# Reciprocal square roots of eighteen norms: Newton steps on VectorE or one power on GpSimd

## The chip, the cores and the metric

The kernel runs on one core of a Trainium2 chip, in one launch. The metric is the device time of a run in microseconds (us). Where several runs were made, the median stands beside the lowest and the highest.

## The reference, cut to what matters

Two streams of tokens, 512 latent and 256 context, 1024 channels each, pass through two layers. A layer norms the stream, projects it into four groups of columns, runs a mixer on each group (SSD, Hyena, retention, S5), projects the four outputs back, and ends with a gated feed-forward stage that is normed too. What the change touches is the factor of each norm:

```python
def rms_norm(x, g):
    xf = x.astype(jnp.float32)
    y = xf * lax.rsqrt(jnp.mean(xf * xf, axis=-1, keepdims=True) + EPS)
    return (y * g.astype(jnp.float32)).astype(x.dtype)

def retention_out(y, g):
    ...
    yn = ((yf - mu) * lax.rsqrt(var + EPS)).astype(g.dtype)
    return (jax.nn.silu(g) * yn).reshape(g.shape[0], g.shape[1], W_GRP)
```

`rms_norm` stands at the two norms of a layer, at the output of the SSD mixer and at the end of the program. The second layer needs no context output, so a few of its context norms are left out.

## The kernel before, in words

Activations lie with channels on the 128 partitions and tokens along the free axis, eight tiles of 128 channels for a stream. Every product of float32 operands is made of three passes of TensorE on rounded high and low parts: ScalarE rounds a tile to its high part (`act`, line 155), VectorE or GpSimd subtracts to get the low part (`sub` over `tt`, line 134). Weights come by SyncE's DMA queue into a staging ring `wst` (line 207) and are split in the same way into `whi` and `wlo`. All matmuls have line 126 and accumulate in PSUM banks of four rings (`ps_mm`, `ps_xa`, `ps_xb`, `ps_md`).

A norm has these steps. The squares of the eight tiles are added into `acc`. TensorE sums `acc` over the partitions with one matmul per 128 tokens against a column of ones (`ps_xa<-const,acc`; in the SSD mixer `sz` stands for `acc`, in the retention `rq`). VectorE scales the sums and adds epsilon, which gives the small tile `rv` (in the retention `rrv`): 128 tokens on the partitions by 2 or 4 groups of tokens, 8 or 16 columns in the retention. `rsq` (line 188) replaces that tile by its reciprocal square root. TensorE then spreads it over all partitions with matmuls against the identity (`ps_xa<-const,rv`), and VectorE multiplies the tiles by the spread row (`nt` in the two norms of a layer, `sin` in the SSD mixer, `ry` in the retention, `xl` in the final norm of `finish`). ScalarE and the low-part subtractions make the operands `ahl`, `alol` (latent) and `ahc`, `aloc` (context) of the next products.

`rsq` takes an integer estimate and three Newton steps, twelve VectorE instructions on the small tile, each of which needs the one before or one of the two before:

```python
self.ts(i, v.bitcast(I32), 1, op0=ALU.logical_shift_right)
self.ts(i, i, -1.0, float(0x5F3759DF), ALU.mult, ALU.add)
self.ts(h, v, -0.5)
y = i.bitcast(F32)
for _ in range(3):
    self.mul(t, y, y)
    self.mul(t, t, h)
    self.stt(v, t, 1.5, y, ALU.add, ALU.mult)
    y = v
```

It is called eighteen times: twice in `start` (context, then latent input), eight times from `norm_seg` (three after the first output projection, three at the entry of the second layer, two after the second output projection; a call takes 256 tokens), three times each in `ssd` and `ret`, and twice in `finish`.

`start` (from line 427) also makes the modulation: weights `wst<-in_wm_dram` go straight to TensorE as `ps_md<-wst,csil`, ScalarE copies the row (`mrow`), TensorE turns it into a column, VectorE adds the bias (`modv`), and only then are two channel tiles of each stream normed. The ring `ps_md` has one bank. Beside that, VectorE makes the tables of the S5 mixer's rotations (`rot`, `rotT`, `rotw`, `s5z`, `early`), which are read later.

The order of the instructions on each engine is not the order of the code. A scheduler places them by the priorities given in the code and by its own estimates of when operands are ready, so another instruction at one place can shift its neighbours on every engine. Each engine then runs its row in order and waits at a row whose operands are missing. Buffers of a ring and PSUM banks add waits of the same kind.

Of the kernel before, what the change touches and what calls it, by code (L numbers as in the profile page):

```python
# [33 lines left out]
def halves(a):  # L34
    """A table as two float32 parts that float32r carries exactly."""
    def keep12(x):
        u = np.ascontiguousarray(x, np.float32).view(np.uint32).astype(np.uint64)
        return ((u + 2047 + ((u >> 12) & 1)) >> 12 << 12).astype(np.uint32).view(np.float32)
    hi = keep12(a)
    return np.ascontiguousarray(np.stack([hi, keep12(a - hi)], 1))  # L40
# [66 lines left out]
class Kern:  # L107
# [7 lines left out]
    def at(self, p):  # L115
        """Instructions in this block get priorities from p on."""
# [44 lines left out]
    def pst(self):  # L161
        """A PSUM bank from the ring of the current flow of work."""
# [5 lines left out]
    def pst2(self, fl="mm+xb"):  # L168
        """As pst, from two rings in turn where no mixer runs."""
# [6 lines left out]
    def flow(self, fl, p=None):  # L176
        """Work that takes its banks and small tiles from rings of its own; p: its priority."""
# [10 lines left out]
    def rsq(self, v, n):  # L188
        """v: (128, n) tile, replaced by 1/sqrt(v)."""
        i = self.sm.tile([128, 24], I32, tag="rq_i" + self.fl[:2], name="rq_i", bufs=2)[:, :n]  # L190
        h = self.sm.tile([128, 24], F32, tag="rq_h" + self.fl[:2], name="rq_h", bufs=2)[:, :n]
        t = self.sm.tile([128, 24], F32, tag="rq_t" + self.fl[:2], name="rq_t", bufs=2)[:, :n]
        self.ts(i, v.bitcast(I32), 1, op0=ALU.logical_shift_right)
        self.ts(i, i, -1.0, float(0x5F3759DF), ALU.mult, ALU.add)
        self.ts(h, v, -0.5)
        y = i.bitcast(F32)
        for _ in range(3):
            self.mul(t, y, y)
            self.mul(t, t, h)
            self.stt(v, t, 1.5, y, ALU.add, ALU.mult)  # L200
            y = v

    def piece(self, src, nk, ncol):
        """src: (128, nk * ncol) of a weight laid out by pieces."""
# [5 lines left out]
    def weights(self, srcs, nk=8):  # L210
        """Pieces of 128 columns as high and low parts."""
# [7 lines left out]
    def held(self, src):  # L219
        """Four tiles of rows of a weight with all its columns, src: (8, 128, 512)."""  # L220
# [20 lines left out]
    def bulk(self):  # L241
        """Products that fill the tensor engine come after the mixers' own."""
# [34 lines left out]
    def put_y(self, s, k, t, c0=0):  # L277
        """Keep tile k of the mixers' output: as operands of the output projection where these have room already."""
# [12 lines left out]
    def ytiles(self, s, p):  # L291
        """Tiles that are not written in the order of their making: each has its own place."""
# [3 lines left out]
    def prep(self):  # L296
# [5 lines left out]
        nc.scalar.dma_start(k, A["c_const"])  # L302
        self.ident = k[:, 0:128]
# [30 lines left out]
    def mod(self, i, c0, c1):  # L334
        """Columns 256*c0 .. 256*c1 of the modulation of layer i."""
# [15 lines left out]
    def mod_vec(self, i, cols, both, p):  # L351
        """As mod for tiles of columns, with a column of the weights a row: products and sums on VectorE.
        The context stream has the tiles in both only."""
# [16 lines left out]
    def gains(self, i, part, s, gat):  # L370
        """(1 + scale) * g for a stream; part is 1 or 4."""
# [4 lines left out]
    def sq_acc(self, s, x, acc, first):  # L376
        """acc += x*x"""
# [7 lines left out]
    def rinv_rows(self, s, accs, scale, c0=0, c1=None):  # L385
        """Per-token 1/sqrt(scale * sum over channels + eps), broadcast to all partitions in PSUM."""
# [14 lines left out]
    def segs(self, s):  # L401
        """Ranges of tokens that are normed one after the other, so that products of one hide the norm of the next."""
# [23 lines left out]
    def start(self):  # L426
        """Norm of the inputs and the first two blocks of columns of the first layer's input projection,
        by pairs of channel tiles as their modulation arrives."""
# [1474 lines left out]
```

## Time and profile before

| what | value |
|---|---|
| median of 3 runs | 1917.07 us |
| lowest and highest run | 1908.82 and 1919.6 us |
| profiled execution: span from its first to its last instruction | 1919.5 us |
| profiled execution: time of its own, apart from the span | none is listed |
| TensorE matmuls busy | 1790.1 us (93%) |
| VectorE busy | 1257.5 us (66%), 2941 instructions |
| ScalarE busy | 713.5 us (37%) |
| GpSimd busy | 207.3 us (11%), 273 instructions |
| mean granted TensorE clock | 0.960 of full speed |

An engine's busy time is a sum over stages that have different limits. What an edit in one stage is worth is read where an engine waits: the timeline prints, behind an instruction, how long its engine sat idle before it and what ended that. PE is TensorE, PEld its weight loads, DVE VectorE, ACT ScalarE, POOL GpSimd, SP SyncE.

### The profile page before, as it was taken

Reading aid. Unit: us, or ns where it says so; the run is one execution under the profiler, and the core shown is the slowest. Engines: PE = TensorE matmul, PEld = TensorE weight load, DVE = VectorE, ACT = ScalarE, POOL = GpSimd, SP = SyncE. Lnnn points to the kernel's source line nnn. Section 1 sums busy time; section 2 is a strip of 40 time slices with the busy share of each in tenths; the row PEclk is TensorE's granted clock in tenths of the full one; section 3 lists DMA queues with packets and bytes.
Section 4 is the critical chain, followed back from the end, with each engine's and each line's share of the span. In section 5 each row is a group of like instructions: output and inputs, shape, how many; then the busy total and the mean of one; then the engine's idle time right before and its main releaser. Section 6 shows DMA issues by size and latency. Waiting matters only on the chain.

```text
span 1919.5 us, 28992 instructions
## 1 busy us (share of the span) xinstructions
PE 1790.1 (93%) x10792; PEld 1526.3 (80%) x10792; DVE 1257.5 (66%) x2941; ACT 713.5 (37%) x1390; POOL 207.3 (11%) x273
## 2 busy tenths in 40 slices
PE   3789878898999999999999999989999999999997
PEld 2678767686789888888888989878866888888886
DVE  8788764778858899777665427678576843233336
ACT  4354234555227223212132115514673542222222
POOL 0201121123002000011223000121110000000000
PEclk9899979998899999999999999999997999999998
DMA  6656588765612335656635513565563322222331
GB/s 231 178 138 186 149 180 229 243 192 160 203 56 89 121 123 164 219 190 230 210 113 131 155 44 123 158 207 159 153 201 96 126 73 94 89 96 88 97 101 56
DMA packets 193089, 280.87 MB, mean 146 GB/s; under 512 B 51745, under 2 KB 127837, under 8 KB 192436
## 3 DMA queue, kind: packets, MB, share of 16 engines
q1 hardware_dynamic: 107188, 166.20, 28.5%
q10 hardware_dynamic: 55920, 64.72, 10.9%
q0 software_dynamic: 29840, 48.09, 8.9%
q8 instruction: 85, 1.39, 0.3%
q14 instruction: 56, 0.46, 0.1%
HBM read 235.00 MB, written 43.96 MB: 145 GB/s over the span
## 4 chain that ended last, share of the span: by engine, by line
PE 58%; DVE 11%; issue 8%; DMA 8%; ACT 3%; POOL 1%; ACTq 0%; SPq 0%; DVEq 0%; POOLq 0%
PE ps_mm L126 31%; PE ps_xb L126 20%; PE ps_xa L126 4%; DMA mvw<-in_wmt_dram 4%; PE ps_md L126 2%; DMA wst<-in_wi_dram 1%; ACT L155 1%; DVE mvo L364 1%; DVE wlo L134 1%; DVE gt L134 1%; DVE t L134 1%; DVE g L1499 1%; DVE cst L134 1%; DVE s5tmp L134 1%; ACT whi L155 1%
## 5 line engine op out<-in xcount | busy, mean ns | idle before, releaser
L155 ACT ACTIVATE whi<-wst 128x1024 fp32r<-128x1024 f32 (+3 forms) x226 | 198.9, 917 | 361.5 <-PE ps_mm L126 169.4
L134 DVE TENSOR_TENSOR wlo<-wst,whi 128x1024 fp32r<-128x1024 f32 (+3 forms) x226 | 233.9, 1058 | 83.5 <-ACT whi L155 81.2
L126 PE MATMUL ps_mm<-alol,whi 128*128 128x512 f32 (+1 forms) x688 | 262.7, 383 | 0.4 <-POOL alol L134 0.4
L126 PE MATMUL ps_mm<-ahl,wlo 128*128 128x512 f32 (+1 forms) x688 | 262.3, 382 | 0.0
L126 PE MATMUL ps_mm<-ahl,whi 128*128 128x512 f32 (+1 forms) x688 | 260.9, 383 | 0.3 <-ACT ahl L155 0.2
L126 PE MATMUL ps_mm<-h,whi 128*128 128x512 f32 (+1 forms) x592 | 168.8, 365 | 0.9 <-DVE h L134 0.7
L126 PE MATMUL ps_xb<-ahl,whi 128*128 128x512 f32 (+1 forms) x416 | 154.2, 373 | 3.8 <-ACT ahl L155 3.8
L126 PE MATMUL ps_xb<-ahl,wlo 128*128 128x512 f32 (+1 forms) x416 | 153.8, 370 | 0.0
L126 PE MATMUL ps_xb<-alol,whi 128*128 128x512 f32 (+1 forms) x416 | 153.5, 371 | 0.1
L134 DVE TENSOR_TENSOR sg<-sg,ps_mm 128x512 f32<-128x512 f32 (+1 forms) x70 | 39.9, 570 | 172.9 <-PE ps_mm L126 172.7
L126 PEld LDWEIGHTS ps_mm<-alol,whi 128*128 128x128 f32 x688 | 130.7, 190 | 26.4 <-issue 2.7
L126 PEld LDWEIGHTS ps_mm<-ahl,wlo 128*128 128x128 f32 x688 | 130.7, 190 | 24.5 <-issue 1.1
L126 PEld LDWEIGHTS ps_mm<-ahl,whi 128*128 128x128 f32 x688 | 130.2, 191 | 25.0 <-issue 1.6
L126 PE MATMUL ps_xb<-h,whi 128*128 128x256 f32 (+1 forms) x592 | 129.2, 310 | 0.1
L364 DVE SCALAR_TENSOR_TENSOR mvo<-mvw,crow 128x1024 f32<-128x1024 f32 x80 | 97.8, 1222 | 39.6 <-DMA mvw<-in_wmt_dram 38.7
L126 PE MATMUL ps_mm<-ahc,whi 128*128 128x256 f32 x368 | 107.4, 296 | 13.0 <-ACT whi L155 8.6
L126 PEld LDWEIGHTS ps_mm<-h,whi 128*128 128x128 f32 x592 | 103.7, 188 | 17.5 <-DVE h L134 1.2
L126 PE MATMUL ps_mm<-aloc,whi 128*128 128x256 f32 x368 | 108.2, 295 | 1.0 <-DVE aloc L134 1.0
L126 PE MATMUL ps_mm<-ahc,wlo 128*128 128x256 f32 x368 | 107.1, 293 | 2.0 <-DVE wlo L134 2.0
L126 PEld LDWEIGHTS ps_xb<-h,whi 128*128 128x128 f32 x592 | 98.9, 188 | 11.6 <-issue 1.1
L126 PE MATMUL ps_mm<-h,wlo 128*128 128x512 f32 (+1 forms) x296 | 107.9, 365 | 0.0
L155 ACT ACTIVATE h<-sg 128x512 fp32r<-128x512 f32 (+1 forms) x70 | 37.4, 534 | 161.7 <-DVE sg L134 161.6
(576 smaller groups left out, 4137.3 us busy)
## 6 DMA issues: line engine op xcount, KB each, us to landing
wst<-in_wu_dram SPq DMA_DIRECT2D x88, 512.0 KB
mvw<-in_wmt_dram POOLq DMA_DIRECT2D x56, 512.0 KB, 3.7
wst<-in_wi_dram SPq DMA_DIRECT2D x42, 512.0 KB
wst<-in_wm_dram SPq DMA_DIRECT2D x40, 512.0 KB
wst<-in_wd_dram SPq DMA_DIRECT2D x24, 384.0 KB
ftab<-in_c_ftL_dram POOLq DMA_DIRECT2D x32, 256.0 KB, 5.0
wst<-in_wd_dram SPq DMA_DIRECT2D x32, 256.0 KB
s5rot<-s5r SPq DMA_DIRECT2D x32, 192.0 KB
```

The source lines that it names most:

```text
L126: return self.nc.tensor.matmul(out, lhsT, rhs, start=start, stop=stop)
L134: return (eng or self.nc.vector).tensor_tensor(out, a, b, op=op)
L155: return self.nc.scalar.activation(out, in_, func, bias=bias, scale=scale)
L364: self.nc.vector.scalar_tensor_tensor(o, st, 1.0, crow[:, q], op0=ALU.mult, op1=ALU.mult, accum_out=mv[:, c, q:q + 1])
L1499: nc.vector.tensor_tensor_scan(o, dcy, x, 0.0, ALU.mult, ALU.add)
```

## The change

`rsq` becomes a single GpSimd instruction that raises the small tile to the power of a constant tile, and that constant tile of minus one half is made once at the start. Twelve VectorE instructions at each of eighteen places go, one GpSimd instruction comes.

```diff
     def rsq(self, v, n):
-        i = self.sm.tile([128, 24], I32, tag="rq_i" + self.fl[:2], name="rq_i", bufs=2)[:, :n]
-        h = self.sm.tile([128, 24], F32, tag="rq_h" + self.fl[:2], name="rq_h", bufs=2)[:, :n]
-        t = self.sm.tile([128, 24], F32, tag="rq_t" + self.fl[:2], name="rq_t", bufs=2)[:, :n]
-        self.ts(i, v.bitcast(I32), 1, op0=ALU.logical_shift_right)
-        self.ts(i, i, -1.0, float(0x5F3759DF), ALU.mult, ALU.add)
-        self.ts(h, v, -0.5)
-        y = i.bitcast(F32)
-        for _ in range(3):
-            self.mul(t, y, y)
-            self.mul(t, t, h)
-            self.stt(v, t, 1.5, y, ALU.add, ALU.mult)
-            y = v
+        self.tt(v, v, self.mhalf[:, :n], ALU.pow, self.nc.gpsimd)
...
         nc.scalar.dma_start(k, A["c_const"])
+        self.mhalf = cp.tile([128, 24], F32, name="mhalf")
+        nc.gpsimd.memset(self.mhalf, -0.5)
```

The scheduler gives the rest of the program a new order. Of 9,733 matmul instructions that both programs have, 1,261 stand elsewhere relative to the others, by at most 104 places. On GpSimd the old rows keep their order but for five. Three places show what moved.

The first is VectorE in `start`, at the first norm's way to its first use. Before, the last of the rows between the second Newton step's end and the first `nt` product (`rot` and `rotT` are rotation tables, `wlo` low parts of weights, `early` S5 powers) read:

```order
L152 SCALAR_TENSOR_TENSOR rv<-rq_t,rv 128x2
L134 TENSOR_TENSOR rotT<-rot,rotw 128x128
L134 TENSOR_TENSOR rot<-rot,rotw 128x128
L134 TENSOR_TENSOR rotw<-rotw 128x16
L134 TENSOR_TENSOR rot<-rot,rotT 128x128
```

In the changed order the rows that end with the first two `nt` products are:

```order
L152 SCALAR_TENSOR_TENSOR rotw<-rotw 128x16
L134 TENSOR_TENSOR wlo<-wst,whi 128x8x128
L149 TENSOR_SCALAR rv<-ps_xa 128x4
L134 TENSOR_TENSOR early<-early,s5T 128x256
L134 TENSOR_TENSOR rotT<-rot,rotw 128x32
L134 TENSOR_TENSOR rot<-rot,rotw 128x64
L134 TENSOR_TENSOR nt<-xc,pb 128x256 x2
```

From the row that makes the context's `rv` to the first `nt` product 77 rows lie between before and 24 now; the rotation rows that stood in front now stand behind.

The second is TensorE at the end of the second layer's mixers, where the retention's factors are spread (`ps_md<-const,rrv`) and the SSD mixer's sums and factors follow (`CE` are decays of the entering states, `yhl` and `yol` the operands of the output projection). Before:

```order
L126 MATMUL ps_xa<-CE,Hn 64x128 x8
L126 MATMUL ps_xb<-const,rq 128x2 x2
L126 MATMUL ps_xa<-CE,Hn 64x128 x8
L126 MATMUL ps_md<-const,rrv 64x128 x8
L126 MATMUL ps_xb<-const,rrv 64x128 x8
L126 MATMUL ps_xa<-const,sz 128x1 x8
L126 MATMUL ps_md<-yhl_13753,whi 128x512
```

Now, first the retention's rows and then, some eighty rows on, the SSD mixer's:

```order
L126 MATMUL ps_xa<-sin 128x128
L126 MATMUL ps_md<-const,rrv 64x128 x8
L126 MATMUL ps_xb<-const,rrv 64x128 x8
L126 MATMUL ps_xa<-vd,Bt 64x256
L126 MATMUL ps_xa<-E,xt 64x128 x4
L126 MATMUL ps_md<-yhl_13587,whi 128x512
```

```order
L126 MATMUL ps_mm<-yhl_13590,wlo 128x256
L126 MATMUL ps_xa<-const,sz 128x1 x8
L126 MATMUL ps_xa<-const,rv 128x128 x4
L126 MATMUL ps_xb<-yhl_13585,whi 128x256
```

The retention's factors are spread before the SSD mixer's last products with `CE`, and products of the output projection fill the rows in between; the SSD mixer's own factor now stands directly behind its sums, with the products that read its tiles (`yhl_13585`) directly behind that.

The third is VectorE at the end of the program, where the second half's last products are added (`xl<-ps_mm,modv`), its squares summed (`acc`), and the first half is multiplied by its factor (`xl<-xl,vec,ps_xa`). Before:

```order
L152 SCALAR_TENSOR_TENSOR xl<-ps_mm,modv_87,xl 128x256
L152 SCALAR_TENSOR_TENSOR xl<-xl,vec,ps_xa 128x256 x8
L134 TENSOR_TENSOR acc<-acc,sq 128x256
L149 TENSOR_SCALAR rv<-ps_xa 128x2
```

Now:

```order
L152 SCALAR_TENSOR_TENSOR xl<-xl,vec,ps_xa 128x256 x4
L152 SCALAR_TENSOR_TENSOR xl<-ps_mm,modv_89,xl 128x256
L152 SCALAR_TENSOR_TENSOR xl<-xl,vec,ps_xa 128x256 x4
L152 SCALAR_TENSOR_TENSOR xl<-ps_xb,modv_89,xl 128x256
L134 TENSOR_TENSOR acc<-acc,sq 128x256
L152 SCALAR_TENSOR_TENSOR xl<-ps_mm,modv_89,xl 128x256
L134 TENSOR_TENSOR acc<-acc,sq 128x256 x2
L149 TENSOR_SCALAR rv<-ps_xa 128x2
```

The eight products of the first half's final norm stood behind the last row that reads TensorE; now they stand three such rows earlier.

## Rows read from the trace of the kernel before

**Rows 1.** The page: its span and the line of busy times.
```profile
span 1919.5 us, 28992 instructions
PE 1790.1 (93%) x10792; PEld 1526.3 (80%) x10792; DVE 1257.5 (66%) x2941; ACT 713.5 (37%) x1390; POOL 207.3 (11%) x273
```

**Rows 2.** Busy time by stretch; columns: stretch, length, engines, clock, DMA share, GB/s.
```profile
0.00:50.00 50.00, 18.72 (x108) 11.63 (x109) 42.45 (x252) 22.89 (x50) 1.49 (x7) 1.00 0.65 235
600.00:700.00 100.00, 100.00 (x661) 91.89 (x661) 86.19 (x298) 36.27 (x80) 9.44 (x14) 1.00 0.29 93
1550.00:1900.00 350.00, 350.00 (x1607) 286.62 (x1606) 129.04 (x166) 91.84 (x124) 0.00 (x0) 1.00 0.28 89
```

**Rows 3.** One tile's instructions, rq_t: count, shortest/median/longest ns, first and last start.
```profile
L134 DVE TENSOR_TENSOR rq_t<-rq_t,rq_h x54: 146/161/665, 33.8 to 1911.4; 128x2 f32<-128x2 f32 x36, 128x4 f32<-128x4 f32 x9, 128x16 f32<-128x16 f32 x6, 128x8 f32<-128x8 f32 x3
```

**Rows 4.** Timeline, first norm: start, duration, instruction, idle before it and releaser.
```profile
30.94 0.15 DVE L149 TENSOR_SCALAR rv<-ps_xa 128x2 f32<-128x2 f32 x1
...
35.11 1.21 DVE L134 TENSOR_TENSOR wlo<-wst,whi 128x1024 fp32r<-128x1024 f32 x1
...
39.35 0.80 PE L126 MATMUL ps_xa<-const,rv 128*128 128x128 f32 x2 [9.13 <-DVE rv L152]
...
42.78 0.42 DVE L134 TENSOR_TENSOR nt<-xc,pb 128x256 f32<-128x256 f32 x1
...
44.75 0.65 PE L126 MATMUL ps_md<-wst,csil 128*32 128x256 f32 x4 [0.71 <-DVE modv L134]
```

**Rows 5.** The same stretch: busy times of four microseconds, and SP's next weight loads.
```profile
36.00:40.00 4.00, 0.65 (x3) 0.65 (x4) 4.00 (x28) 0.00 (x0) 0.00 (x0) 1.00 0.00 0
...
45.89 1.49 SPq L207 DMA_DIRECT2D wst<-in_wm_dram  x2
```

**Rows 6.** Timeline, TensorE at the retention's factors of context, layer 1.
```profile
496.31 1.98 PE L126 MATMUL ps_mm<-const,rrv 128*64 128x128 f32 x16 [3.23 <-DVE rrv L152]
```

**Rows 7.** Timeline, TensorE at the end of the second layer's mixers.
```profile
1482.08 1.12 PE L126 MATMUL ps_xa<-CE,Hn 128*64 128x128 f32 x8 [4.45 <-DVE rrv L152]
```

**Rows 8.** Timeline before the second layer's feed-forward stage, and a stretch as in Rows 2.
```profile
1518.02 0.16 DVE L149 TENSOR_SCALAR rv<-ps_xa 128x2 f32<-128x2 f32 x1 [0.18 <-PE ps_xa L126]
...
1526.34 0.68 PE L126 MATMUL ps_xa<-const,rv 128*128 128x128 f32 x4 [1.07 <-DVE rv L152]
1529.66 0.58 PE L126 MATMUL ps_xb<-ahl,whi 128*128 128x256 f32 x1 [2.64 <-ACT ahl L155]
...
1528.00:1532.00 4.00, 2.28 (x9) 1.99 (x10) 4.00 (x8) 3.46 (x8) 1.92 (x2) 0.52 0.58 170
```

**Rows 9.** Timeline, the end of the program.
```profile
1904.11 0.61 PE L126 MATMUL ps_xa<-const,rv 128*128 128x128 f32 x4
1908.46 0.98 PE L126 MATMUL ps_xa<-const,acc 128*128 128x1 f32 x4 [3.74 <-DVE acc L134]
1911.95 1.20 PE L126 MATMUL ps_xa<-const,rv 128*128 128x128 f32 x4 [2.51 <-DVE rv L152]
...
1904.76 3.22 DVE L152 SCALAR_TENSOR_TENSOR xl<-xl,vec,ps_xa 128x256 f32<-128x256 f32 x8
```

**Rows 10.** Groups by shape: count, busy us, mean ns, idle before and releaser.
```profile
L134 POOL TENSOR_TENSOR alol<-nt,ahl 128x256 fp32r<-128x256 f32 x24 | 19.0, 790 | 123.6 <-ACT ahl L155 123.6
L1885 POOL MEMSET const-float32-0.0<- 128x1 f32 x1 | 0.1, 99 | 0.3 <-issue 0.3
...
L134 DVE TENSOR_TENSOR alol<-nt,ahl 128x256 fp32r<-128x256 f32 x24 | 12.4, 518 | 4.8 <-ACT ahl L155 4.6
```

**Rows 11.** Timeline: a hand-off from VectorE to GpSimd, and GpSimd's first arithmetic.
```profile
357.24 0.68 DVE L134 TENSOR_TENSOR t<-vp,Ft 128x512 f32<-128x512 f32 x1
...
358.07 1.06 POOL L134 TENSOR_TENSOR t<-t,t 128x256 f32<-128x256 f32 x1 [0.77 <-DVE t L134]
...
44.91 0.73 POOL L134 TENSOR_TENSOR aloc<-nt,ahc 128x256 fp32r<-128x256 f32 x1 [43.55 <-ACT ahc L155]
```

**Rows 12.** The chain that ended last, in order of time: start, us, what.
```profile
1901.43 1.43 PE ps_xb L126 x12
```

## The prediction

> **What bounds the kernel now.** I read the page's busy times first, then busy time by stretch, then the timeline around each of the eighteen norms. TensorE is busy for 1790.1 of 1919.5 us [rows 1], so all that an edit elsewhere can give back is some 130 us of TensorE's idle time, plus matmuls that ran at a lower clock behind such idle time. Two of the long stretches show TensorE busy without a gap (100.00 of 100.00 us from 600, 350.00 of 350.00 us from 1550) [rows 2]; a norm that falls there costs nothing now, however long its chain. The first 50 us are another matter: TensorE 18.72 us busy, VectorE 42.45 [rows 2]. So the question is at which of the eighteen places TensorE stands still because of the Newton steps.
>
> It does at six. In `start` the context's sums are turned into `rv` at 30.94, and TensorE spreads it at 39.35 after 9.13 us of idleness that VectorE's `rv` ended [rows 4]. A lone chain of twelve takes about 2.1 us; here its rows were queued among rotation tables and low parts. TensorE's next instructions are behind it, the modulation among them, which runs at 44.75 [rows 4], so no weight buffer comes free: the DMA share of 36 to 40 us is 0.00 and the next weight loads are issued at 45.89 [rows 5]. The retention of the context stream holds TensorE for 3.23 us [rows 6], the end of the second layer's mixers for 4.45 us [rows 7], the norm ahead of the last feed-forward stage for 1.07 and then 2.64 us [rows 8], and the end of the program for 3.74 and 2.51 us [rows 9].
>
> **The change, part by part.** *Removed:* 12 x 18 = 216 VectorE instructions of about 0.161 us [rows 3], some 35 us of VectorE's 1257.5. Where TensorE has no gaps this is worth nothing, since VectorE has room there (86.19 of 100, 129.04 of 350) [rows 2]. I count it at nothing except where VectorE is the engine that is late.
>
> *Added:* eighteen powers and one fill of a small tile. No row shows a power on GpSimd. From below it costs the 0.10 us of the smallest fill; from above, twelve steps at the 0.79 us of a subtraction of 128x256 would be 9.5 us [rows 10]. I take 0.8 us: a subtraction over 256 columns fits into 0.79 us, and a power has 2 to 16 columns and perhaps a dozen or two elementary steps for each, so the same number of steps. The new path is then: VectorE's `rv` 0.16, hand-off to GpSimd 0.15 (357.24 + 0.68 to 358.07 [rows 11]), the power 0.8, hand-off to TensorE about 0.15, in all 1.3 us against 2.5 for a lone chain [rows 9].
>
> GpSimd works at 790 ns where VectorE takes 518 for the same shape [rows 10]. The Trainium skill's page "GPSIMD Engine Reference", section "Engine selection", says to keep elementwise arithmetic on VectorE, because GpSimd takes about twice as long for operations with two inputs. The trace agrees in direction, with a ratio of 1.5. By that rule alone the change loses at every place; by the rows one instruction stands against twelve, so the ratio would have to exceed about twelve.
>
> *GpSimd's queue:* each power stands where its operand is due. At the entry of the feed-forward stages it stands behind four low parts of the segment before, which end ahead of the old time of spreading, so I count that wait at nothing; the cover is the product work in TensorE's queue. Its DMA issues (the modulation weights of the second layer) move behind the context's power by less than the old order made them wait.
>
> *Covered places:* in the changed order eleven norms have 20 to 37 matmuls between sums and spreading, mostly 28. At 1.43 us for 12 [rows 12] 28 last 3.3 us, above the path of 1.3. They cost and give nothing.
>
> *The first norm.* `rv` ready at 30.94 + 1.3 is spread at about 32.2 instead of 39.35. Next VectorE is late: 24 rows lie before the first `nt` now. The second `wlo` starts at 35.11 before [rows 4]; less six Newton rows spaced 0.08 us and plus four short rows behind it, `nt` starts at about 36.4, not 42.78. The modulation, and with it the loads of 45.89 [rows 5], come about 6.5 us earlier. But the rotation rows that stood in front follow behind, and VectorE is busy throughout (4.00 of 4.00 [rows 5]). If it stays the bound, only the 24 Newton rows of both norms are won, 24 x 0.075 = 1.8 us; if its later gaps take in the tables, 6.7 us. Taken: 4.5.
>
> *The retention of the context:* 2.5 us becomes 1.3; 1.2 won (0 to 1.5).
>
> *The end of the second layer's mixers.* The 4.45 us [rows 7] go, since the retention's spreading no longer follows the products with `CE`. What is late next is the SSD mixer: its factor is spread right behind its sums and its tiles are read right behind that, so 1.3 us of path, about 0.7 for the product and 0.6 for the rounding lie open. Won: 4.45 - 2.6, less 0.4 for the spreading itself, 1.5 (-1 to 4.5).
>
> *The norm before the last feed-forward stage.* Twelve rows among sums and `wlo` took from 1518.02 to 1526.34 [rows 8]. With a path of 1.3 us and 28 matmuls as cover, the operands are ready when TensorE arrives, and 1.07 + 2.64 us go; behind that gap the granted clock was 0.52 [rows 8], which lost another 1 to 3 us. Taken: 4 (1 to 7).
>
> *The end.* Before, TensorE ends its products at 1904.1, the eight products of the first half take 3.22 us on VectorE and the last sum waits for them; TensorE idles 3.74 us [rows 9]. Now these products start once 28 matmuls have passed, with some 3.1 us of matmuls left; about 5.4 us of VectorE rows then end 2.3 us behind TensorE instead of 4.2, less 0.2 for the spreading moved: 1.7 won. The lone chain gives 2.5 - 1.3 = 1.2. Together 2.9 (0 to 5.5).
>
> **The sum.** 4.5 + 1.2 + 1.5 + 4 + 2.9 = 14.1 us, with ends of about 3 and 25. Against the profiled execution: 1919.5 - 14.1 = 1905.4. The median of the runs lies 2.4 us below its span, so for a median I forecast **1903 us**. About 0.5% (9.6 us) is what a measurement of this kernel can tell from no change.
>
> **The rivals.**
>
> *The power is long (slower).* GpSimd would have to take more than about 2.8 us, so that 2.8 + 0.5 us of hand-offs outlast the 3.3 us of the 28 matmuls. From there each of the eleven covered places holds TensorE for the excess, and four open ones for what passes 2 us. At 4.5 us that is 11 x 1.7 + 4 x 2.5 = 29 us less some 4 still won at the first norm: 25 slower, about 1942; at the upper end of 9.5 us about 2020. For it: nothing in the trace prices the operation. Against it: the sizes are 2 to 16 columns, and 0.79 us buys 256 subtractions.
>
> *VectorE or the loads are the bound anyway.* The stalls go, but the next wait takes their place: 1.8 at the first norm, 1.2, 0, 1 and 2.9 at the others, 6.9 in all, about 1910. For it: VectorE without a gap in `start` [rows 5], and `wlo` rows in the queue before the feed-forward stage. The new order elsewhere can add or take a few us with either sign.
>
> *The first power is slow to begin.* If code for it had to be loaded when first called, the first norm would be spread about when it is now, and 4.5 us less are won: about 1907.5. Against it: GpSimd's first arithmetic instruction took 0.73 us, like later ones [rows 11]. The Trainium skill's page "GPSIMD Engine Reference", section "Instruction dispatch", puts such a load at roughly 6 us for the first call of a freshly loaded routine. By that figure the sum would be the same 1907.5 or so; the trace shows no such delay for a subtraction.
>
> That the change does not do what it says is out: its VectorE order has no Newton rows left, and its GpSimd order has eighteen powers.
>
> **How the numbers follow.** My forecast has 0.54 (own range 1894 to 1912), the bound elsewhere 0.24 (1905 to 1922), the slow first call 0.06, the long power 0.16 (1922 to 2020). The range is 1894 to 1922: it leaves out the long power and the far end of the largest gains, 2 in 10. Faster by over 0.5% (below 1907.5): four fifths of the forecast, half of the slow first call, a little of the second rival, 0.50. Slower by over 0.5% (above 1926.7): nearly all of the long power, 0.16. The rest, 0.34, lies between.
>
> **What would show it.** In the profile of the changed kernel a power group on GpSimd of 18 instructions should have a mean near 0.8 us; above 2.8 the first rival holds. The wait of TensorE at the first spreading should fall from 9.13 to about 2 us and the third pair of weight loads should be issued near 39 instead of 45.89. TensorE's gap ahead of the last feed-forward stage should be under 1 us with the clock at 1.00 there. VectorE's busy time should fall by about 35 us, and TensorE's stretches without gaps should stay so. I am wrong if TensorE waits for GpSimd at the covered places, or if the first modulation comes early and the first products of the feed-forward stage or of the second block of columns do not.

## The result, and the profile after

| | before | changed |
|---|---|---|
| median of 9 runs | 1917.07 us | 1926.58 us |
| lowest and highest | 1908.82 and 1919.84 us | 1920.95 and 1936.18 us |
| span of the profiled execution | 1919.5 us | 1926.7 us |

The ratio is 1.0052, with a 95% interval of 1.0035 to 1.007: half a per cent slower, 4.6 us beyond the upper end of the range.

The page of the changed kernel, against [rows 1]:

```profile
span 1926.7 us, 28815 instructions
PE 1790.1 (93%) x10792; PEld 1523.7 (79%) x10792; DVE 1228.1 (64%) x2725; ACT 711.5 (37%) x1390; POOL 235.4 (12%) x292
```

TensorE is busy for the same 1790.1 us as before. All of the 7.2 us by which the spans differ is TensorE's idle time, although VectorE lost 29.4 us of work. The powers, in GpSimd's groups by shape (count, busy us, mean ns, idle before and releaser):

```profile
L134 POOL TENSOR_TENSOR rv<-rv,mhalf 128x2 f32<-128x2 f32 x12 | 9.6, 799 | 479.7 <-DVE rv L149 448.9 <-DVE s5z L134 30.8
L134 POOL TENSOR_TENSOR rrv<-rrv,mhalf 128x16 f32<-128x16 f32 x2 | 5.8, 2914 | 72.8 <-DVE rrv L148 72.8
L134 POOL TENSOR_TENSOR rv<-rv,mhalf 128x4 f32<-128x4 f32 x3 | 3.2, 1072 | 55.5 <-DVE rv L149 55.5
L134 POOL TENSOR_TENSOR rrv<-rrv,mhalf 128x8 f32<-128x8 f32 x1 | 1.6, 1637 | 8.3 <-DVE rrv L148 8.3
```

The guess of 0.8 us holds for two columns and not beyond: each further column adds about 0.15 us ((2.914 - 0.799) / 14).

**Where the time goes.** To see at which place the executions part, I lined them up by the work that TensorE had done: every matmul counted at the shortest spacing that its form usually shows in the two traces, and for each amount of work the time at which each execution reached it. The difference is called the lag below; it is worked out from the two traces and is no row of either. The changed kernel is 12.5 us ahead at 58 us of its span, 0.9 ahead at 91, 4.7 ahead at 385, 0.9 behind at 599, 4.4 ahead at 1406, 12.2 behind at 1534, 10.1 behind from 1583 to 1911, and 7.2 behind at the end. Between 385 and 599 it loses 5.6 us and has won 5.3 back by 1406; the stretch from 1406 to 1534 loses 16.6 us, more than the whole difference.

The start (timeline: start, duration, instruction, idle before it and releaser), against [rows 4, 5]:

```profile
32.20 0.70 POOL L134 TENSOR_TENSOR rv<-rv,mhalf 128x2 f32<-128x2 f32 x1 [30.79 <-DVE s5z L134]
32.95 0.79 PE L126 MATMUL ps_xa<-const,rv 128*128 128x128 f32 x2 [1.78 <-POOL rv L134]
37.50 0.75 DVE L134 TENSOR_TENSOR nt<-xc,pb 128x256 f32<-128x256 f32 x2
40.27 1.94 PE L126 MATMUL ps_md<-wst,csil 128*32 128x256 f32 x16
41.41 8.56 SPq L196 DMA_DIRECT2D wst<-in_wm_dram  x3
```

The wait of 9.13 us is 1.78, and the weight loads are issued 4.48 us earlier (45.89 to 41.41; the prediction had them near 39). In this execution most of the lead is gone at 91 us (timeline, then busy time by stretch as in [rows 2]):

```profile
81.60 7.57 POOL L134 TENSOR_TENSOR aloc<-nt,ahc 128x256 fp32r<-128x256 f32 x1 [13.07 <-ACT ahc L155]
...
89.22 0.58 PE L126 MATMUL ps_mm<-aloc,whi 128*128 128x256 f32 x1 [5.57 <-POOL aloc L134]
...
84.00:88.00 4.00, 0.00 (x0) 0.00 (x0) 4.00 (x12) 0.00 (x0) 4.00 (x1) 0.50 0.14 50
```

A subtraction that takes 0.79 us elsewhere [rows 10] takes 7.57 on GpSimd while VectorE, with rows of the S5 tables (`cst`, `s5M`, `W`), is busy 4.00 of 4.00 us; TensorE waits 5.57 us for it, and its granted clock is 0.50 from 80 to 92 us, the lower of its two levels.

The second layer's mixers. SyncE's queue before, and after it (start, duration of the issue, what):

```profile
1432.73 0.37 SPq L897 DMA_DIRECT2D E<-acd1l  x1
...
1450.32 0.38 SPq L897 DMA_DIRECT2D E<-acd1l  x1
...
1476.28 2.57 SPq L964 DMA_DIRECT2D CE<-acd1l  x4
```

```profile
1456.56 0.33 SPq L196 DMA_DIRECT2D wst<-in_wo_dram  x1
1457.17 0.38 SPq L216 DMA_DIRECT2D wst<-in_wo_dram  x1
1459.67 8.41 SPq L888 DMA_DIRECT2D E<-acd1l  x2
...
1489.38 0.97 SPq L216 DMA_DIRECT2D wst<-in_wo_dram  x2
1491.04 2.58 SPq L955 DMA_DIRECT2D CE<-acd1l  x4
```

`E` and `CE` are the decays of the latent SSD mixer, read from DRAM. The third load of `E` comes 27 us later, the last loads of `CE` 15 us later; weights of the output projection now stand ahead of both. These weights are not what held them: each of the two rings has two buffers, and a load leaves when TensorE has read the tile that it replaces. The first eight products with `E` end at 1432.64 before and at 1459.64 now, and the third load of `E` is issued at 1432.73 and at 1459.67; the last loads of `CE` follow the first products with `CE` by 1.1 and 0.7 us. TensorE's products with `E` and `CE`, before and then after (count, shortest/median/longest ns, first and last start):

```profile
L126 PE MATMUL ps_xa<-E,xt x32: 272/273/473, 1432.0 to 1470.6; 128*64 128x128 f32 x32
L126 PE MATMUL ps_xa<-CE,Hn x32: 420/422/477, 1475.2 to 1483.9; 128*64 128x128 f32 x32
```

```profile
L126 PE MATMUL ps_xa<-E,xt x32: 272/273/421, 1457.0 to 1482.8; 128*64 128x128 f32 x32
L126 PE MATMUL ps_xa<-CE,Hn x32: 272/273/323, 1490.3 to 1501.4; 128*64 128x128 f32 x32
```

So the loads are late because the products ahead of them are. In TensorE's row the first product with `E` stands 112 places later than before and the first with `CE` 62, and of the output projection's 288 products 126 instead of 48 stand ahead of the SSD mixer's sums. ScalarE sat 7.7 us before its first row on the first `E`. What TensorE then waits for, at the mixer's end:

```profile
1499.77 0.66 PE L126 MATMUL ps_xa<-CE,Hn 128*64 128x128 f32 x8 [1.15 <-issue]
1501.04 0.66 PE L126 MATMUL ps_xa<-CE,Hn 128*64 128x128 f32 x8 [0.62 <-PE ps_xa L126]
...
1505.98 0.38 PE L126 MATMUL ps_xa<-const,sz 128*128 128x1 f32 x2 [2.45 <-ACT sz L155]
1506.58 3.11 PE L126 MATMUL ps_xa<-const,sz 128*128 128x1 f32 x14 [0.22 <-ACT sz L155]
1511.05 2.08 PE L126 MATMUL ps_xa<-const,rv 128*128 128x128 f32 x8 [1.35 <-POOL rv L134]
1514.70 0.58 PE L126 MATMUL ps_xb<-yhl,whi 128*128 128x256 f32 x1 [1.57 <-ACT yhl L155]
```

The retention was spread at 1477.91. Between the SSD mixer's sums and the spreading of its factor 12 products of the output projection stood before and none stands now, so nothing covers its last steps: 7.4 us of waits in these rows, 1.35 of them for the power. The chain of waits goes from TensorE's products to the loads that follow them:

```profile
1467.09 0.61 PE ps_xa L126 x8
1467.72 5.41 DMA E<-acd1l
...
1490.41 1.05 PE ps_xa L126 x16
1491.68 0.61 SPq L955
...
1493.01 6.48 DMA CE<-acd1l
```

These waits are not the whole 16.6 us. Over the stretch TensorE is idle for 21.1 us where it was 9.6; 9.8 of the 21.1 lie between 1418 and 1437, at a reload of the retention (4.72), the SSD mixer's `dtt` (1.83) and the retention's state (3.22). The rest is the same products at a lower clock: 107.3 us busy instead of 102.4, with a granted clock of 0.50 from 1510 to 1520.

Elsewhere the terms came out. The first layer's retention of context waits 1.98 us instead of 3.23 [rows 6], the products behind the spreading before the last feed-forward stage follow without a gap [rows 8], and the two waits at the end are 2.81 and 1.10 instead of 3.74 and 2.51 [rows 9]:

```profile
494.55 1.97 PE L126 MATMUL ps_mm<-const,rrv 128*64 128x128 f32 x16 [1.98 <-POOL rrv L134]
...
1533.77 0.60 PE L126 MATMUL ps_xa<-const,rv 128*128 128x128 f32 x4
...
1917.06 0.99 PE L126 MATMUL ps_xa<-const,acc 128*128 128x1 f32 x4 [2.81 <-DVE acc L134]
1919.15 1.23 PE L126 MATMUL ps_xa<-const,rv 128*128 128x128 f32 x4 [1.10 <-POOL rv L134]
```

### The profile page after: what moved, and what is told of

Its sections match the earlier page's. It is cut to its first block, busy times and chain, and to the rows that moved or that the text cites. A ratio compares the mean times of both kernels' runs of the same rounds, so it can differ in the third digit from the quotient of the medians.

```text
span 1926.7 us, 28815 instructions
## 1 busy us (share of the span) xinstructions
PE 1790.1 (93%) x10792; PEld 1523.7 (79%) x10792; DVE 1228.1 (64%) x2725; ACT 711.5 (37%) x1390; POOL 235.4 (12%) x292
```

## The experiments

Theory: the power saves time where it stands, and the order that the scheduler makes around it loses more, above all by late loads of the SSD mixer. Rivals: the power is long; every wait that goes is waited for again; any edit moves the time. Ratios are against runs of the kernel before on the same chip (medians of 1914.65 to 1919.02 us). Lags are gained within a stretch: "start" up to 92 us, "first mixers" 389 to 506 us, "second mixers" 1411 to 1523 us, all by the clock of before; "behind" is from there to the end. They come from one execution each, and the stretches between are left out.

Three things limit what a lag can show. In e4, whose rows on TensorE, VectorE and SyncE are those of before, it reaches -3.3, so some 3 us is no finding. The stretches left out weigh as much as those shown: e15's four columns add up to -14.2 and its span is 7.2 us shorter. And the executions of e7 and e8 that were profiled (1908.93 and 1917.21 us) are the fastest of their kernels, some 8 us below the medians. In e10, e14 and e16 the lag also jumps by 3 to 4.5 us between 1521 and 1525 us, so the edge decides which of the last two columns has it.

| run | norm | ratio (95%) | start | first mixers | second mixers | behind |
|---|---|---|---|---|---|---|
| changed kernel | power | 1.0052 (1.0035 to 1.007) | -0.9 | +3.2 | +16.6 | -5.0 |
| e1 | power twice | 1.007 (1.0044 to 1.0096) | -1.2 | +21.8 | -0.6 | -2.2 |
| e2 | power but at second mixers | 1.0044 (1.0026 to 1.0063) | -9.4 | +6.9 | +13.3 | -6.9 |
| e3 | power at second mixers only | 1.0009 (0.9993 to 1.0025) | -1.9 | -0.4 | -3.9 | +1.6 |
| e4 | Newton and the fill | 0.9991 (0.9977 to 1.0006) | +0.1 | -2.1 | -0.2 | +0.1 |
| e5 | power in start only | 1.0084 (1.0062 to 1.0106) | -7.9 | +14.3 | +0.3 | 0.0 |
| e6 | power but in start | 1.0079 (1.0055 to 1.0103) | -1.3 | +3.8 | +16.8 | -4.3 |
| e7 | power, loads moved | 0.9997 (0.9981 to 1.0012) | -8.3 | +3.5 | +1.9 | -6.3 |
| e8 | power at both ends | 1.0044 (1.0021 to 1.0067) | -7.6 | +9.6 | -3.8 | -4.4 |
| e9 | power, low parts moved | 1.0068 (1.0048 to 1.0088) | -1.3 | +7.0 | +17.2 | -5.3 |
| e10 | Newton, loads moved | 1.0036 (1.0024 to 1.0048) | -0.5 | +0.5 | +5.2 | -1.7 |
| e11 | power, loads moved twice | 1.0089 (1.0065 to 1.0114) | -8.6 | +20.6 | +7.2 | -4.6 |
| e12 | e11 and e9 | 1.0069 (1.005 to 1.0088) | -2.6 | +15.8 | +5.7 | -4.8 |
| e13 | power, order of before | 0.9987 (0.997 to 1.0003) | -1.1 | -0.5 | -1.1 | -1.5 |
| e14 | Newton, changed order | 1.0224 (1.02 to 1.0248) | -1.1 | +6.6 | +17.6 | -0.5 |
| e15 | power, spliced order | 0.9968 (0.9949 to 0.9986) | -9.3 | -2.5 | +1.4 | -3.8 |
| e16 | Newton, spliced order | 1.006 (1.0038 to 1.0082) | +4.4 | +0.3 | +0.5 | +1.2 |
| e17 | power twice, order of before | 1.0035 (1.0018 to 1.0053) | -0.8 | +0.2 | -0.6 | -0.6 |
| e18 | power, second splice | 0.9964 (0.9944 to 0.9985) | -8.2 | -0.1 | -4.1 | -5.1 |

### The power doubled, or taken away where time was lost

e1, e2, e3 (the calls are counted in the order of the code) and e4, on the kernel before:

```diff
e1 +        self.tt(v, v, self.pone[:, :n], ALU.pow, self.nc.gpsimd)
e2 +        if not (self.nq not in (12, 13)): return self.newton(v, n)
e3 +        if not (self.nq in (12, 13)): return self.newton(v, n)
e4 +        nc.gpsimd.memset(self.mhalf, -0.5)
```

> The changed kernel with a second power (exponent 1) behind each of the eighteen, so GpSimd's work at every norm doubles; the order in which the scheduler lays SyncE's queue at the second layer's mixers comes out as in the kernel before (the third and fourth loads of the SSD mixer's E stand ahead of the last output-projection weights again). Theory 'order' (what the changed kernel lost is the late SSD mixer at 1500 to 1515 us, because its loads stand behind weight loads): the 14 us lost there come back, the second power costs at the open places 0.7 to 2.9 us each, some 6 us; 1916 to 1922, faster than the changed kernel's 1926.6, and TensorE's waits between 1495 and 1515 fall from 8 us to under 3. Rival 'the power is long': what was lost is the power's own time, so it doubles: 1932 to 1945.

> Newton steps again in the second layer's SSD and retention mixers, the power at the other sixteen norms. SyncE's queue keeps the changed kernel's place for the third and fourth E (behind the output-projection weights), only the last four CE stand ahead of two more weight loads. Theory 'order': the SSD mixer is still late and most of the loss stays: 1920 to 1928. Rival 'the power is long': the loss between 1470 and 1515 us goes with the two powers there: 1909 to 1915.

> The power only in the second layer's SSD and retention mixers, Newton steps at the other sixteen norms; SyncE's queue there is that of the kernel before. Theory 'order': no loss, 1914 to 1919, within 0.2% of the kernel before. Rival 'the power is long': the loss of the changed kernel is made by these two powers (2.9 and 1.0 us), 1926 to 1933.

> The kernel before with nothing but the unused constant tile and its fill added. Theory 'order': the rows keep their order on every engine, so 1917 within 2 us. Rival 'any edit moves it': a median more than 4 us from that of the kernel before with no power and no Newton step changed.

e1 gave 1930.87 us, between both expectations, and its total told nothing; its place did. With twice the power but the order of before there (SyncE's queue, and the SSD mixer's places in TensorE's row), the second mixers lose nothing (-0.6), and a new loss of 21.8 stands at the first layer's mixers, which the theory had not foreseen. e2, with Newton steps back at the place of the loss, loses 13.3 there (1925.87 us), though its last four `CE` stand ahead of the weights. e3, with the power there and the old order, loses nothing (1919.06). So the power at these two norms is not what holds TensorE there. e4 (1916.62) shows that an edit that moves no row changes nothing beyond the interval.

### One half of the change at a time, and the late loads moved

```diff
e5 +        if not (self.nq < 2): return self.newton(v, n)
e6 +        if not (self.nq > 1): return self.newton(v, n)
e7 -            nc.sync.dma_start(e, ...)
e7 +            (nc.gpsimd if lat and i else nc.sync).dma_start(e, ...)
e7 -                nc.sync.dma_start(ce[64 * r:64 * r + 64], ...)
e7 +                (nc.gpsimd if lat and i else nc.sync).dma_start(ce[64 * r:64 * r + 64], ...)
e8 +        if not (self.nq < 2 or self.nq > 13): return self.newton(v, n)
```

> The power only at the two norms of the program's start, Newton steps at the other sixteen; TensorE's order differs from the kernel before in the first third and in some 500 rows of the second layer's output projection, SyncE's queue at the second layer's mixers is that of the kernel before. Theory 'order': the first norm's wait goes and is kept or partly given back before 100 us, and nothing is lost at the second layer's mixers: 1907 to 1915. Rival 'every saved wait is waited for again': 1915 to 1919.

> The reverse: Newton steps at the two norms of the start, the power at the other sixteen; at the second layer's mixers the order is that of the changed kernel on TensorE and SyncE. Theory 'order': the late SSD mixer stays, with no gain at the start: 1924 to 1932, not faster than the changed kernel's 1926.6. Rival 'what was lost is lost in the start' (VectorE and GpSimd hindering each other between 80 and 90 us): 1914 to 1918.

> The changed kernel, power at all eighteen norms, with one thing moved: the loads of E and CE of the second layer's latent SSD mixer are issued by GpSimd's queue instead of SyncE's, where they stood behind weight loads. TensorE's and VectorE's order up to the second layer's mixers is the changed kernel's row for row. Theory 'order': the SSD mixer ends some 10 us earlier relative to the retention, 1912 to 1918, 9 to 14 us under the changed kernel. Rival 'the power is long': no change, 1924 to 1929.

> The power where nothing but the scheduler's local order changes: the two norms of the start, the two ahead of the last feed-forward stage and the two of the program's end; Newton steps at the twelve between. SyncE's queue at the second layer's mixers is that of the kernel before. Theory 'order': the three gains seen in the changed kernel (start, 3.4 us ahead of the last feed-forward stage, 2.9 us at the end) without its loss: 1902 to 1912. Rival 'every saved wait is waited for again': 1914 to 1919.

e7 gave 1917.44 us: with every power in place and the same order up to the second mixers, the loss there is 1.9 instead of 16.6 once the loads of `E` and `CE` are out of SyncE's queue. That the loads alone did it is not shown. With them TensorE's, VectorE's and ScalarE's rows inside the mixers moved too: the first product with `E` stands 36 places earlier than in the changed kernel, and 22 products lie between the SSD mixer's sums and the spreading where none did. GpSimd's queue issues the last four `CE` at 1471.03 instead of 1491.04, behind TensorE's products as before:

```profile
1454.31 0.91 POOL L888 DMA_DIRECT2D E<-acd1l  x1 [2.46 <-PE ps_xa L126]
1471.03 2.51 POOL L955 DMA_DIRECT2D CE<-acd1l  x4 [1.14 <-PE ps_xa L126]
```

e6 (1934.4) keeps the loss of 16.8 with no gain in the start, a little beyond its upper end of 1932. e5 (1931.62) and e8 (1924.83) missed by 13 to 17 us: the lead at the start is there (-7.9, -7.6), and 14.3 and 9.6 are lost at the first mixers. There loads of the SSD mixer come later, in e5 the first `CE` at 393.29, right behind a weight load, where before had 387.77; that this costs the 14.3 us is not shown:

```profile
377.66 15.57 SPq L215 DMA_DIRECT2D wst<-in_wi_dram  x2
393.29 0.61 SPq L974 DMA_DIRECT2D CE<-acd0l  x1
```

### Repairs, and a control

```diff
e9  -                    self.sub(lo, t, hi, None if k % 2 else nc.gpsimd)
e9  +                    self.sub(lo, t, hi)
e10, on the kernel before: the two lines of e7
e11 as e7, with (nc.gpsimd if lat else nc.sync)
e12 = e11 and e9
```

> The changed kernel with one thing moved in the program's start: the low parts that GpSimd made there (eight, of every second channel tile) are made by VectorE. From the second half of the first layer on TensorE's order is the changed kernel's. In the changed kernel's profile one of these, 128x256, took 7.57 us from 81.60 on, the last 7 us beside rows of VectorE that followed each other without a gap, and TensorE waited 5.57 us for it; in the profile of the kernel with the moved loads, of the same order in the start, it took 1.74. Theory 'GpSimd shut out': the gain of the first norm is then kept, the lag behind the kernel before at 100 us is -6 to -10 instead of -1, and the median falls by 2 to 6: 1920 to 1925. Rival 'VectorE is the bound of the start': eight more rows of 0.42 to 0.68 us on VectorE cost what they last, 1926 to 1931.

> The kernel before, Newton steps everywhere, with the loads of E and CE of the second layer's latent SSD mixer on GpSimd's queue: the same move that took the changed kernel from 1926.6 to 1917.4. Theory 'order': in the kernel before these loads were not late, so it gains little, 1913 to 1918. Rival 'the move is worth 9 us by itself': 1905 to 1911, and the power would still be 9 us behind.

> The changed kernel with these loads of the latent SSD mixer on GpSimd's queue in both layers. The first layer lost 4 us at the same place between 470 and 490 us (lag behind the kernel before -4.7 to -0.5). Theory 'order': these come back too, 1911 to 1917. Rival 'only the second layer's were late': as with the second layer's alone, 1916 to 1919.

> The last two together: loads of the SSD mixer on GpSimd's queue in both layers and the start's low parts on VectorE, power at all eighteen norms. If both causes are right the predicted gain is there: 1906 to 1914, faster than the kernel before by 0.2 to 0.6%. If either gain is waited for again later: 1915 to 1920.

All four were slower than the kernel before (1931.8, 1925.8, 1934.94, 1932.05 us). e10 is the control for e7 and lies above both of its expectations: the move, with the new order that comes with it, makes the kernel before 0.36% slower, so GpSimd's queue is not the better place by itself. e9's start ends at -1.3 as the changed kernel's does, and its time lies just above the rival's range: no gain from the low parts on VectorE. In e11 and e12, which have e7's move too, the second mixers lose 7.2 and 5.7, and the same move in the first layer costs 15.8 to 20.6 at the first mixers: the expectation was wrong there, and why was not followed up. By now ten of the twelve kernels with a new order (all so far but e4) lay 0.36 to 0.89% above the kernel before, whatever their norm. Order and norm had to be parted.

### The order held, the norm changed

The order of a kernel is recorded as each instruction's place on its engine, and pinned in another (`own` holds the norm's own rows, which stay free):

```diff
+    def pin_order(self):
+        ins = [i for i in ... if i.name not in self.own]
+        for i, x in zip(ins, d):
+            row = rows.setdefault(str(i.engine), [])
+            row.append((len(row) + int(x), i))
+        for row in rows.values():
+            row.sort(key=lambda r: r[0])
+            for (_, a), (_, b) in zip(row, row[1:]):
+                self.tc.add_manual_dep(b, a.name, ...)
```

The edges order the issue on one engine and are meant to add no wait for another; a kernel pinned to its own order, which would show that pinning costs nothing, was not run. e13 pins the order of before, e14 that of the changed kernel, e15 and e16 a spliced one.

> The power at all eighteen norms, but every other instruction pinned to the place that it has on its engine in the kernel before (all five engines' rows are those of before, less the 216 Newton rows, plus the eighteen powers and the fill). Theory 'order' (the power by itself saves time and the new order loses more): 1906 to 1913, 2 to 6 us from the start, some 1 at the first layer's retention, some 2 ahead of the last feed-forward stage, 2.4 at the end. Rival 'the power costs time where it stands': 1919 or more. Rival 'every saved wait is waited for again': 1915 to 1919.

> The reverse: Newton steps at all eighteen norms, every other instruction pinned to its place in the changed kernel. Theory 'order': the order's loss without the power's gain, 1930 to 1938, slower than the changed kernel's 1926.6. Rival 'the power costs time': 1912 to 1918, the changed kernel's order without its powers is as fast as the kernel before or faster.

> The power at all eighteen norms and an order put together of two: up to TensorE's 1,120th product and from its 7,660th on that of the kernel with the power at both ends (which kept 8 us at the start and won 6 at the last output projection and the end), between them that of the kernel before. Theory 'order': both gains and no loss between, 1900 to 1909, faster than the kernel before by 0.4% or more. If a gain of the start is waited for again in the old order behind it: 1910 to 1917.

> The same spliced order with Newton steps at all eighteen norms: what the power adds when the order is held. Theory 'order' with a saving of the power of its own: 4 to 12 us above the spliced kernel with the power. Rival 'the order is all': within 2 us of it.

| | order of before | changed order | spliced order |
|---|---|---|---|
| Newton steps | 1 | 1.0224 | 1.006 |
| power | 0.9987 | 1.0052 | 0.9968 |

In each column the power is the better one: by 0.13% where the order was made for Newton steps (its interval reaches 1.0003), by 1.7% and 0.9% where it was made for powers. With the power, the changed order costs 0.65% over that of before, some 12 us. e14 (1962.69) is 25 us beyond its expectation, since Newton steps in rows laid out for a power hold TensorE in many places (35.1 us in 16 waits for a norm's factor, 7.5 in six with the powers); at the second mixers it loses 17.6, as with powers. e15 at 1913.14 is faster than both kernels and lies in its second range, where a gain of the start is waited for again: of 9.3 us at 92 us 2.0 are left at 389. e16 (1930.79) is 17.7 us above e15, beyond both of its expectations.

e13 (1914.66), 1.7 us above its range, also shows two readings wrong. In the start the power is there at 32 us and the early modulation is not, since VectorE's rows are as before: TensorE waits 6.26 us one step later, and the loads are issued at 44.97, 0.9 us earlier and not 4.5. And the wait at the second mixers stays, with the power in place:

```profile
41.51 1.01 PE L126 MATMUL ps_md<-const,mrow 128*128 128x2 f32 x4 [6.26 <-ACT mrow L155]
...
44.97 10.74 SPq L196 DMA_DIRECT2D wst<-in_wm_dram  x4
...
1477.24 1.12 PE L126 MATMUL ps_xa<-CE,Hn 128*64 128x128 f32 x8 [4.61 <-DVE CE L134]
```

In the kernel before the same wait bore the name of `rrv` [rows 7]. ScalarE's row in that trace says what it was; the load had left at 1476.28, behind the products with the first two `CE`, which start at 1475.2:

```profile
1480.63 0.63 ACT L155 ACTIVATE CE<-CE 128x512 f32<-128x512 f32 x1 [4.41 <-DMA CE<-acd1l]
```

### The price of the power, and a better splice

```diff
e17, on e13: +        self.own.add(self.tt(v, v, self.pone[:, :n], ALU.pow, self.nc.gpsimd).ins.name)
e18, on e15: the last part (from TensorE's 7,640th product) of the order with powers at both ends and in the second mixers
```

> The kernel of e13 (order of the kernel before, power at all eighteen norms) with a second power, of exponent 1, behind each: GpSimd's time at every norm doubles and nothing else moves. Theory 'order': covered norms hide it, the open ones pay 0.7 to 1.6 us each (two in the start, the first layer's retention, the end), 2 to 6 us above e13's 1914.7, so 1916 to 1921. Rival 'the power is long': every norm pays, 0.7 x 12 + 1.1 x 3 + 1.6 + 2 x 2.9, some 19 us, 1930 to 1936.

> As the spliced kernel e15, but its last part (from TensorE's 7,640th product on) is the order that the scheduler gave the kernel with the power at both ends and in the second layer's mixers. The run with the power in the second layer's mixers alone won 4 us there in its profile, the spliced kernel nothing. If that gain is a matter of the order: 1905 to 1911. If not: as e15, 1911 to 1915.

e17 gave 1921.25 us, by ratio 0.48% or 9 us above e13, between the expectations. The profiles show who pays: in e13 the retention of 16 columns ahead of the first feed-forward stage held TensorE for 0.62 us, with the second power for 3.57. Its cover was at its end with one power:

```profile
570.60 3.01 PE L126 MATMUL ps_xa<-const,rrv 128*64 128x128 f32 x32 [3.57 <-POOL rrv L134]
```

e18, at 1907.57 us beside 1914.65 for the kernel before, ratio 0.9964, is the fastest version of the study: powers at all eighteen norms, 8.2 us won in the start, 4.1 at the second mixers, 5.1 behind, and no loss at the first; 4.4 of the first 8.2 are lost again by 389 us. It differs from e15 by no more than the intervals (0.9944 to 0.9985, and 0.9949 to 0.9986).

## Why the prediction was wrong

*The power's time.* Right for two columns (0.80), too small for 8 and 16 (1.64, 2.91). In the changed kernel no covered place was held for more than 0.62 us. VectorE's busy time fell by 29.4 us, not 35. "The power is long" did not happen, and it was the only rival that ended slower.

*The first norm.* The mechanism was right as far as the loads: the 9.13 us went to 1.78, VectorE's rows decided, the loads came 4.5 us earlier (some 6.5 were forecast). How much of it lasts is open. The long subtraction was not foreseen, but it is the exception: seven other kernels (e2, e5, e7, e8, e11, e15, e18) have the same first 420 rows on VectorE and 500 on TensorE, their subtraction took 0.90 to 1.75 us, and they are 7.6 to 9.4 us ahead at 92 us. By 150 us all eight are 2.1 to 6.2 us ahead, the changed kernel 4.2, about the 4.5 taken. That this is the power's is not shown: e13, with the old order there, is 5.6 us ahead at 389, and e3, with Newton steps in the start, 5.1.

*The retention of context, the norm ahead of the last feed-forward stage, the end.* Forecast 1.2, 4 and 2.9. The first was 1.25 (3.23 less 1.98), the second 3.4 in the lag, of which 1.4 came back behind it, the third 2.9 (10.1 less 7.2).

*The end of the second layer's mixers.* Here the prediction fell. It took 1.5 us as won (-1 to 4.5) where 16.6 were lost. Two steps failed. It took the 4.45 us of [rows 7] for Newton's because the wait had the name of `rrv`; ScalarE's row of the same stretch (1480.63, above) shows a load of `CE`, and e13 keeps 4.61 without Newton steps. And it priced the SSD mixer's new place as 2.6 us, from the last rows alone ("its factor is spread right behind its sums"), and did not ask when the operands of these rows arrive. They arrive late because the whole mixer stands later in the new order: its first products with `E` 112 places, those with `CE` 62, and each load of a further `E` or `CE` leaves only behind them. At the mixer's end 7.4 us lay open instead of 2.6; 9.8 us of idleness around 1430 and the lower clock, which make up most of the rest, had no term at all.

*The new order.* "Can add or take a few us with either sign" was a clause in a rival. The five kernels with the changed order at the second mixers (changed, e2, e6, e9, e14) lose 13.3 to 17.6 us there, with power or Newton steps; the ten with the old order there lie between -4.1 and +1.4. So it is the order that costs. Which part of it does is not parted: the five have SyncE's new order and TensorE's new places together (32 products with `CE` behind the retention's spreading), the ten have neither (none to 4).

*What stays open.* The loss at the first layer's mixers (3 to 22 us) goes with the order too: it is absent in e3, e10 and e13 and from e15 on, with powers and with Newton steps. That late loads make it is argued from e5's queue only, and the one repair tried there made it worse. At the second mixers no run moved the SSD mixer's rows on TensorE without the loads, or the loads without the rows.

## What to carry to other kernels

Where a scheduler lays out the program, an edit has two effects, its own and that of the new order, and the second can be the larger: here 0.13% gained, not clear of noise, and 0.65% lost. Read the difference of order on every engine, and ask of each load that comes later what released it, the load ahead of it in its queue or the instruction that frees its buffer. To learn what an edit is worth, pin the old order and change the edit alone, then pin the new order and undo it.

## What the runs showed of the hardware

A GpSimd subtraction of 128x256 took 7.57 us (7.75 and 7.68 in e1 and e16) beside VectorE rows with both inputs in SBUF that followed each other without a gap, and 1.74 in e7, where VectorE had paused 0.26 us for a load. The Trainium skill, page "SBUF — State Buffer", section "Who interferes with whom", says that a VectorE instruction with two inputs in SBUF contends with a GpSimd instruction that reads SBUF. The traces agree, and show GpSimd waiting out some twenty instructions in a row. It need not come so: in e2, e15 and e18, with the same rows and no pause, the subtraction took 0.90 to 0.94 us, and two VectorE rows beside it took 1.36 to 1.38 us where they take 0.82 or 0.83. What decides who goes first was not tested.

The first power of a program took 0.70 us (at 32.20), like later ones of two columns; no slow first call is seen.
